# Values of attention heads 2 and 3 computed in one pass of 512-column products, with their weights kept

## The chip, the cores and the metric

The kernel runs on one core of a Trainium2 chip. The metric is the device time of one execution in microseconds. TensorE (PE) does the matrix products, ScalarE (ACT) casts and activations, VectorE (DVE) and GpSimd (POOL) elementwise work; SyncE (SP) issues the transfers that matter here.

## The reference

One layer of an encoder block on 1024 tokens of 1024 features: a combined input projection, gated linear attention in two directions (4 heads, key size 128, value size 256), a pooling branch, a gated merge, and an FFN. The part that the change touches is the value projection of heads 2 and 3 and what is put around it:

```python
h = rmsnorm(x, norm_mix[l])
proj = h @ w_in[l]
q, k, v, r, lr_f, lr_b, u, g_a, g_b = jnp.split(proj, split_points, axis=-1)
...
vh = to_heads(v, GLA_HEADS)
...
scores = jnp.einsum('bhncd,bhnsd->bhncs', q_e, k_e)
scores = jnp.where(mask, scores, 0.0)
o_intra = jnp.einsum('bhncs,bhnse->bhnce', scores, v)
kv = jnp.einsum('bhnsd,bhnse->bhnde', k_d, v)
...
o = (o * jax.nn.silu(r.astype(jnp.float32))).astype(x.dtype)
y_a = o @ w_branch_gla[l]
```

## The kernel before

**Products.** Every large product is made three times in a reduced-precision fp32 format: each operand is split into a hi part and a lo part, and hi x hi, hi x lo and lo x hi are summed in PSUM (`products`, L274; `mm3` calls it and then the queue, see below). The split is made by `split_to`: a cast on ACT (L200) gives hi, a subtraction gives lo (L201, on POOL for weights, on DVE for data). A token tile is 128 tokens (8 of them, `t`), a k-tile is 128 of the 1024 features (8 of them). One `mm3` of 512 columns is one unit of the queue.

**The queue.** TensorE's order is fixed when the program is written. After each `mm3`, `pump(dt)` (dt = 1 for 512 columns, 0.5 for 256) advances several lists:

- `side`: the attention of a head, a generator that yields after each piece how many units to wait until the next. `begin(attention(h, q, k))` puts it in. It first makes decays and their exponentials (its prelude, about 35 units, among them `qe` and `fac` on POOL, L809 and L810, scans on DVE, L778, exponentials on ACT, L798 to L800, key transposes `kp` on PE, L826), then waits until the values of its head are there (`while h not in v_heads: yield 0.5`), then makes 7 backward steps (`advance`, 1.2 units each: the product `kv`, the state `st` on DVE, L838 and L840, and its scaled copies `sb`, `sf`, `so` on ACT, L844 and L848), the scores (`sc`, `p`) and 8 forward steps (`op` in PSUM, the last product of each taking the scaled state `sf`, L922). About 59 units in all.
- `pending`: weight splits of the next projection, one popped every two units. `prepare` loads a weight (raw tiles, 4 buffers) and queues its splits; `take` hands out a weight, makes its remaining splits at once, and prepares the next one.
- `aside`: the work of `branch_jobs` (sums of the branch's weights: `wsum` on POOL, L706), advanced only while `pending` is empty, at a spacing given in units.

All engines work in the order in which the instructions are written, so a split or cast stands behind whatever was written before it on its engine.

**Heads.** The values of heads 0 and 1 are made together by `pair_products` (512 columns: 256 for each head), with attention(0) beside them; their results are split by two casts on ACT (L507) and two subtractions on DVE (L509) for each token tile. Then, for h = 1, 2, 3, `project_qk` makes q and k (2 x 16 units), `begin(attention(h, ...))` queues the head's attention, and for h = 2 and 3 `values` makes the head's own values, 8 tiles of 8 k-tiles with 256 columns each. In this manner attention(0) runs beside the pair products and head 1's projection, attention(1) beside head 2's projection and values, attention(2) beside head 3's.

**The r stage** follows: 8 weights of 128 columns (`j`), 2 halves of 8 units each. From j = 3 on each half is gated (`gated`: Silu on ACT, L1097, four transposes on PE, L1100, a product on DVE, L1107); the halves of j < 3 are stored and gated later (`put_by`). attention(3) runs into this stage.

Of the kernel before, what the change touches and what calls it, by code (L numbers as in the profile page):

```python
# [10 lines left out]
F32 = mybir.dt.float32  # L11
# [42 lines left out]
def kernel(  # L54
# [38 lines left out]
    def name(s):  # L93
        count[0] += 1
        return f"{s}_{count[0]}"

    def slot(dtype=F32, shape=(2, HALF), s="slot"):
        return slots.tile([P, *shape], dtype, tag="slot", name=name(s))
# [10 lines left out]
    def bank(pool, s="ps"):  # L109
        return pool.tile([P, HALF], F32, tag=pool.name, name=name(s))  # L110

    def as_f32(ap):
        return ap.bitcast(F32)
# [85 lines left out]
    def split_to(hi, lo, src, eng=nc.vector):  # L199
        nc.scalar.copy(hi, src)  # L200
        eng.tensor_tensor(lo, src, as_f32(hi), op=ALU.subtract)  # L201
# [35 lines left out]

    order = []
    for h in range(HEADS):
        cols_of = [(Q0 + h * DK, DK), (K0 + h * DK, DK), (V0 + h * DV, DV)]  # L240
        order += [(w_in, KT, *c) for c in cols_of[: 2 if h < 2 else 3]]
    order += [(w_in, KT, R0 + j * P, P) for j in range(KT)]
    order = iter(order)
    loaded, ready = [], []
# [14 lines left out]
    def take(ahead=True):  # L259

        if not ready:
            prepare()
        w = ready.pop(0)
        w.finish()
        if ahead:
            prepare()
        return w
# [8 lines left out]
    def mm3(ps, a, b, first, last, onto=False):  # L276
        products(ps, a, b, first, last, onto)
        pump(ps.shape[-1] / HALF)
# [15 lines left out]
    def tokens(pair, t):  # L294
        return tuple(p[:, (t % 4) * P : (t % 4 + 1) * P] for p in pair)
# [123 lines left out]
            norm_x(t)  # L419
            yield 2  # L420

    def values(w, v, t):
        ps = bank(ps_mm)
        for kt in range(KT):
            mm3(ps[:, :DV], tokens(hT(kt, t // 4), t), w(kt), kt == 0, kt == KT - 1)
        split_to(*(part[:, t % 4, :] for part in v[t // 4]), ps[:, :DV])

    lw = [wts.tile([P, 4, 4, 2 * RANK], F32R, tag="wh", name=name("lw")) for _ in range(2)]
    up = slot(F32R, (HEADS, 2, DK), "up")

    def low_rank_weights():
# [3 lines left out]
            nc.vector.tensor_tensor(lw[i][:, :, 3, :], raw, as_f32(lw[i][:, :, 0, :]), op=ALU.subtract)  # L438
        nc.scalar.copy(up[:, :, :, :], uraw[:, :, :, :])
        nc.vector.tensor_tensor(up[32:64], uraw[32:64], as_f32(up[32:64]), op=ALU.subtract)  # L440

    def value_slots():
        return [(slot(F32R, (4, DV), "vh"), slot(F32R, (4, DV), "vl")) for _ in range(2)]

    cols = const.tile([P, 40], F32, tag="cols", name="cols")

# [41 lines left out]
    split_pair_weight()  # L488
    for kp in range(2):
        transpose_tile(trs[kp], xn[1], 1, kp)  # L490
    pair_v = [[], []]

    def pair_products(ts, before=None):
        banks = [bank(ps_mm) for _ in ts]
        for k in range(KT):
            if before:
                before(k)
            for ps, t in zip(banks, ts):
                mm3(ps[:, :], tokens(hT(k, t // 4), t), pair_w[k], k == 0, k == KT - 1)
        for ps, t in zip(banks, ts):  # L500
            for h in range(2):
                if t // 4 == len(pair_v[h]):
                    pair_v[h].append((slot(F32R, (4, DV), "vh"), slot(F32R, (4, DV), "vl")))
            parts = [[part[:, t % 4, :] for part in v[t // 4]] for v in pair_v]
            halves = [ps[:, h * DV : (h + 1) * DV] for h in range(2)]
            for (hi, _), src in zip(parts, halves):
                nc.scalar.copy(hi, src)  # L507
            for (hi, lo), src in zip(parts, halves):
                nc.vector.tensor_tensor(lo, src, as_f32(hi), op=ALU.subtract)  # L509

    def first_steps(k):
        if k == 2:
# [214 lines left out]
    v_heads, o_heads, unscaled = {}, {}, []  # L727
    HOLD, SCORES = 4.4, 6

    def project_qk():  # L730
        q = slot(s="q")
        k = slot(s="k")
        for dst, scale in ((q, DK**-0.5), (k, 1.0)):
            w = take()
            for half in range(2):
                ps = feature_major(w, hT, half)
                nc.scalar.activation(dst[:, half, :], ps[:, :], AF.Copy, scale=scale)
        return q, k
# [220 lines left out]
    def first_qk():  # L959
        q, k = slot(s="q"), slot(s="k")  # L960
        low_rank(0)
        weights = [take()]
        for half in range(2):
            if half:
                finish_side()
                low_rank(1)
                prepare()
            for n, (dst, scale) in enumerate(((q, DK**-0.5), (k, 1.0))):
                if n == len(weights):
                    weights.append(take(ahead=False))  # L970
                ps = feature_major(weights[n], hT, half)
                nc.scalar.activation(dst[:, half, :], ps[:, :], AF.Copy, scale=scale)
        return q, k

    for h in range(HEADS):
        qk = project_qk() if h else first_qk()
        begin(attention(h, *qk))
        if h == 0:
            for ts in ((7,), (6,), (5, 4)):
                pair_products(ts)  # L980
            v_heads.update(enumerate(pair_v))
            prepare_beside(map(branch_jobs, range(4)), 5)
        if h > 1:
            v = value_slots()
            w = take()
            for t in range(NT):
                values(w, v, t)
            v_heads[h] = v

    class Unit:  # L990

# [1041 lines left out]
```

## Time and profile before

| | us |
|---|---|
| median of 3 runs | 1380.25 (1379.61 to 1381.26) |
| the profiled execution | 1380.1 |
| its span | 1378.1 |
| TensorE busy | 1367.6 |
| values of head 2 begin on TensorE | 154.3 |
| first gated Silu on ACT | 321.8 |

In a row of the timeline stand the start in us from the span's start, the duration, engine, line, operation, output and inputs, the shapes, how many rows were joined (x), and in brackets how long the engine had been idle and what released it. Durations of matmuls are pipelined latencies, so they overlap; the distance between two starts is what a product costs.

### The profile page before, as it was taken

The page shows a single profiled execution, that of the slowest core. Times are in us where ns is not written, and L with a number is a line of the kernel's source. Part 1 is how long each engine was busy: PE and PEld are TensorE (multiplying, and loading weights), DVE is VectorE, ACT ScalarE, POOL GpSimd, SP SyncE. Part 2 cuts the span into 40 slices and gives each one's busy share as a digit, 9 for nine tenths or more (in the row PEclk, how much of TensorE's full clock was granted, in tenths as well). Part 3 has the DMA queues.
Part 4 walks back from the last instruction along what each step waited for, and adds up shares of the span by engine and source line. Part 5 has one row for each costly group of instructions (what it writes and reads, how often), then busy time and mean ns, then how long its engine had stood idle before and what let it go on. Part 6 is the DMA issues. An engine that isn't in the chain of part 4 may idle for free. (4 is left out here: it accounts for less than half of the span.)

```text
span 1378.1 us, 18207 instructions
## 1 busy us (share of the span) xinstructions
PE 1367.6 (99%) x6514; PEld 1147.4 (83%) x6514; DVE 839.8 (61%) x1027; ACT 642.6 (47%) x1170; POOL 750.7 (54%) x554
## 2 busy tenths in 40 slices
PE   9999999999999999999999999999999999999998
PEld 7888899988888888888888888888888888888886
DVE  6364656557745876688883955656656556343375
ACT  7375666655334445554347533333333334444353
POOL 3222617132297646668665276666666667455454
PEclk9999999999999999999999999999999999999999
DMA  6121413312478678996516355555544447985561
GB/s 226 31 62 47 147 62 125 110 48 77 138 230 278 197 229 277 371 394 216 175 61 245 115 176 176 176 176 176 165 143 139 144 136 266 385 306 186 170 214 77
DMA packets 166586, 243.60 MB, mean 177 GB/s; under 512 B 10936, under 2 KB 95968, under 8 KB 166496
## 3 DMA queue, kind: packets, MB, share of 16 engines
q1 hardware_dynamic: 166352, 242.18, 52.3%
q8 instruction: 51, 0.84, 0.3%
q14 instruction: 39, 0.32, 0.1%
q10 hardware_dynamic: 144, 0.26, 0.1%
HBM read 164.55 MB, written 77.86 MB: 176 GB/s over the span
## 5 line engine op out<-in xcount | busy, mean ns | idle before, releaser
L201 POOL TENSOR_TENSOR wl<-fs,wh 128x512 fp32r<-128x512 f32 x120 | 167.6, 1400 | 157.2 <-ACT wh L200 103.2
L274 PE MATMUL ps<-gh,wh 128*128 128x512 f32 x616 | 240.9, 391 | 0.0
L274 PE MATMUL ps<-gl,wh 128*128 128x512 f32 x616 | 240.2, 390 | 0.3 <-DVE gl L1591 0.3
L274 PE MATMUL ps<-gh,wl 128*128 128x512 f32 x616 | 240.0, 390 | 0.0
L201 POOL TENSOR_TENSOR wl<-fraw,wh 128x512 fp32r<-128x512 f32 x90 | 129.7, 1441 | 63.6 <-ACT wh L200 61.2
L274 PE MATMUL ps<-hh,wh 128*128 128x512 f32 x376 | 151.9, 404 | 0.0
L201 POOL TENSOR_TENSOR ol<-gor,oh 128x1024 fp32r<-128x1024 f32 (+1 forms) x42 | 101.7, 2425 | 85.7 <-ACT oh L200 59.6
L274 PE MATMUL ps<-hh,wl 128*128 128x512 f32 x376 | 146.9, 391 | 0.0
L274 PE MATMUL ps<-hl,wh 128*128 128x512 f32 x376 | 146.8, 390 | 0.0
L274 PEld LDWEIGHTS ps<-gl,wh 128*128 128x128 f32 x616 | 115.8, 188 | 24.1 <-DVE gl L1591 0.7
L274 PEld LDWEIGHTS ps<-gh,wh 128*128 128x128 f32 x616 | 115.8, 188 | 24.0 <-ACT hb L1610 0.3
L274 PEld LDWEIGHTS ps<-gh,wl 128*128 128x128 f32 x616 | 115.7, 188 | 24.1
L201 POOL TENSOR_TENSOR wl<-raw,wh 128x512 fp32r<-128x512 f32 x40 | 54.7, 1379 | 121.9 <-ACT wh L200 103.5
L274 PE MATMUL ps<-oh,oh 128*128 128x512 f32 x308 | 120.0, 390 | 0.0
L274 PE MATMUL ps<-oh,ol 128*128 128x512 f32 x308 | 120.0, 390 | 0.0
L274 PE MATMUL ps<-ol,oh 128*128 128x512 f32 x308 | 120.0, 389 | 0.0
L201 POOL TENSOR_TENSOR wl<-wraw,wh 128x512 fp32r<-128x512 f32 x56 | 92.2, 1675 | 44.7 <-ACT wh L200 44.5
L201 DVE TENSOR_TENSOR ol<-wor,oh 128x1024 fp32r<-128x1024 f32 (+1 forms) x42 | 62.8, 1506 | 68.1 <-ACT oh L200 55.5
L200 ACT CAST wh<-fs 128x512 fp32r<-128x512 f32 x120 | 73.8, 615 | 26.1 <-DVE fs L1010 25.1
L274 PEld LDWEIGHTS ps<-hh,wl 128*128 128x128 f32 x376 | 70.6, 188 | 15.0
L274 PEld LDWEIGHTS ps<-hl,wh 128*128 128x128 f32 x376 | 70.9, 188 | 12.9
L274 PEld LDWEIGHTS ps<-hh,wh 128*128 128x128 f32 x376 | 70.8, 188 | 12.8
(279 smaller groups left out, 3126.3 us busy)
## 6 DMA issues: line engine op xcount, KB each, us to landing
fraw<-in_w_ffn_in_dram SPq DMA_DIRECT2D x44, 512.0 KB, 7.2
gor<-g_out SPq DMA_DIRECT2D x35, 512.0 KB, 5.8
g_out<-s SPq DMA_DIRECT2D x44, 256.0 KB, 2.3
raw<-in_w_in_dram SPq DMA_DIRECT2D x40, 256.0 KB, 5.1
fraw<-in_w_in_dram SPq DMA_DIRECT2D x20, 512.0 KB, 7.1
wor<-t_out SPq DMA_DIRECT2D x20, 512.0 KB, 4.5
g_out<-g SPq DMA_DIRECT2D x33, 256.0 KB, 2.5
x<-in_x_dram SPq DMA_DIRECT2D x16, 512.0 KB, 4.5
```

Of the source, the lines that this page charges most:

```text
L200: nc.scalar.copy(hi, src)
L201: eng.tensor_tensor(lo, src, as_f32(hi), op=ALU.subtract)
L274: nc.tensor.matmul(ps, a[i], b[j], start=first and n == 0, stop=last and n == 2, skip_group_check=onto)
```

## The change

The values of heads 2 and 3 are computed in one pass behind head 2's q and k projection. `ValueWeights` loads eight k-tiles of 512 columns (256 KB each), four of them when head 2's k-projection begins and the others as splits are made; it splits six of them while that projection runs (through `pending`) and the last two in the first token tile. Two of the k-tiles (6 and 7) are kept in slots, because the pools `wh` and `wl` have six buffers. `products` makes 8 token tiles of 8 products of 512 columns, from t = 7 to t = 0, and `keep_values` (also used by `pair_products`) splits each result into the values of the two heads. The q weights of head 3 are prepared in the last token tile (t = 0, third k-tile) instead of a whole projection ahead. attention(2) is queued ahead of the products but gets its values only when all are made; attention(3) is queued behind head 3's projection, with the r stage right behind. The branch jobs are queued as two and two, spaced 3.7 and 4 units instead of 5. In all 384 products of 256 columns become 192 of 512.

```diff
@@ -237,8 +237,7 @@
 
     order = []
     for h in range(HEADS):
-        cols_of = [(Q0 + h * DK, DK), (K0 + h * DK, DK), (V0 + h * DV, DV)]
-        order += [(w_in, KT, *c) for c in cols_of[: 2 if h < 2 else 3]]
+        order += [(w_in, KT, c + h * DK, DK) for c in (Q0, K0)]
     order += [(w_in, KT, R0 + j * P, P) for j in range(KT)]
     order = iter(order)
     loaded, ready = [], []
@@ -419,15 +418,6 @@
             norm_x(t)
             yield 2
 
-    def values(w, v, t):
-        ps = bank(ps_mm)
-        for kt in range(KT):
-            mm3(ps[:, :DV], tokens(hT(kt, t // 4), t), w(kt), kt == 0, kt == KT - 1)
-        split_to(*(part[:, t % 4, :] for part in v[t // 4]), ps[:, :DV])
-
-
-
-
     lw = [wts.tile([P, 4, 4, 2 * RANK], F32R, tag="wh", name=name("lw")) for _ in range(2)]
     up = slot(F32R, (HEADS, 2, DK), "up")
 
@@ -438,9 +428,6 @@
             nc.vector.tensor_tensor(lw[i][:, :, 3, :], raw, as_f32(lw[i][:, :, 0, :]), op=ALU.subtract)
         nc.scalar.copy(up[:, :, :, :], uraw[:, :, :, :])
         nc.vector.tensor_tensor(up[32:64], uraw[32:64], as_f32(up[32:64]), op=ALU.subtract)
-
-    def value_slots():
-        return [(slot(F32R, (4, DV), "vh"), slot(F32R, (4, DV), "vl")) for _ in range(2)]
 
     cols = const.tile([P, 40], F32, tag="cols", name="cols")
 
@@ -488,7 +475,18 @@
     split_pair_weight()
     for kp in range(2):
         transpose_tile(trs[kp], xn[1], 1, kp)
-    pair_v = [[], []]
+    pair_v = {}, {}
+
+    def keep_values(vs, t, ps):
+        for v in vs:
+            if t // 4 not in v:
+                v[t // 4] = slot(F32R, (4, DV), "vh"), slot(F32R, (4, DV), "vl")
+        parts = [[part[:, t % 4, :] for part in v[t // 4]] for v in vs]
+        halves = [ps[:, h * DV : (h + 1) * DV] for h in range(2)]
+        for (hi, _), src in zip(parts, halves):
+            nc.scalar.copy(hi, src)
+        for (hi, lo), src in zip(parts, halves):
+            nc.vector.tensor_tensor(lo, src, as_f32(hi), op=ALU.subtract)
 
     def pair_products(ts, before=None):
         banks = [bank(ps_mm) for _ in ts]
@@ -498,15 +496,7 @@
             for ps, t in zip(banks, ts):
                 mm3(ps[:, :], tokens(hT(k, t // 4), t), pair_w[k], k == 0, k == KT - 1)
         for ps, t in zip(banks, ts):
-            for h in range(2):
-                if t // 4 == len(pair_v[h]):
-                    pair_v[h].append((slot(F32R, (4, DV), "vh"), slot(F32R, (4, DV), "vl")))
-            parts = [[part[:, t % 4, :] for part in v[t // 4]] for v in pair_v]
-            halves = [ps[:, h * DV : (h + 1) * DV] for h in range(2)]
-            for (hi, _), src in zip(parts, halves):
-                nc.scalar.copy(hi, src)
-            for (hi, lo), src in zip(parts, halves):
-                nc.vector.tensor_tensor(lo, src, as_f32(hi), op=ALU.subtract)
+            keep_values(pair_v, t, ps)
 
     def first_steps(k):
         if k == 2:
@@ -727,11 +717,64 @@
     v_heads, o_heads, unscaled = {}, {}, []
     HOLD, SCORES = 4.4, 6
 
-    def project_qk():
+    class ValueWeights:
+
+
+        ORDER = (0, 1, 2, 3, 6, 7, 4, 5)
+        IN_SLOTS = (6, 7)
+
+        def __init__(self):
+            self.raw, self.parts = [], {}
+            for _ in range(4):
+                self.load()
+            pending.append(self.split)
+            pending.extend([self.next] * 5)
+
+        def load(self):
+            k = self.ORDER[len(self.raw)]
+            raw = wts.tile([P, HALF], F32, tag="raw", name=name("raw"), bufs=4)
+            nc.sync.dma_start(raw[:, :], w_in[k * P : (k + 1) * P, V0 + 2 * DV : V0 + 4 * DV])
+            self.raw.append(raw)
+
+        def split(self):
+            n = len(self.parts)
+            k = self.ORDER[n]
+            if k in self.IN_SLOTS:
+                w = slot(F32R, s="wv")
+                parts = w[:, 0, :], w[:, 1, :]
+            else:
+                parts = [wts.tile([P, HALF], F32R, tag=s, name=name(s))[:, :] for s in ("wh", "wl")]
+            split_to(*parts, self.raw[n][:, :], nc.gpsimd)
+            self.parts[k] = parts
+
+        def next(self):
+            if len(self.raw) < KT:
+                self.load()
+            self.split()
+
+        def products(self):
+            while pending:
+                pending.pop(0)()
+            vs = {}, {}
+            for t in reversed(range(NT)):
+                ps = bank(ps_mm)
+                for n, k in enumerate(self.ORDER):
+                    if t == NT - 1 and n in (0, 1):
+                        self.next()
+                    elif t == 0 and n == 2:
+                        prepare()
+                    mm3(ps[:, :], tokens(hT(k, t // 4), t), self.parts[k], n == 0, n == KT - 1)
+                keep_values(vs, t, ps)
+            return vs
+
+    def project_qk(last=False):
         q = slot(s="q")
         k = slot(s="k")
         for dst, scale in ((q, DK**-0.5), (k, 1.0)):
-            w = take()
+            final = last and dst is k
+            w = take(not final)
+            if final:
+                value_weights.append(ValueWeights())
             for half in range(2):
                 ps = feature_major(w, hT, half)
                 nc.scalar.activation(dst[:, half, :], ps[:, :], AF.Copy, scale=scale)
@@ -972,20 +1015,18 @@
                 nc.scalar.activation(dst[:, half, :], ps[:, :], AF.Copy, scale=scale)
         return q, k
 
+    value_weights = []
     for h in range(HEADS):
-        qk = project_qk() if h else first_qk()
+        qk = project_qk(h == 2) if h else first_qk()
         begin(attention(h, *qk))
         if h == 0:
             for ts in ((7,), (6,), (5, 4)):
                 pair_products(ts)
             v_heads.update(enumerate(pair_v))
-            prepare_beside(map(branch_jobs, range(4)), 5)
-        if h > 1:
-            v = value_slots()
-            w = take()
-            for t in range(NT):
-                values(w, v, t)
-            v_heads[h] = v
+            prepare_beside(map(branch_jobs, range(2)), 3.7)
+        if h == 2:
+            v_heads.update(zip((2, 3), value_weights.pop().products()))
+            prepare_beside(map(branch_jobs, range(2, 4)), 4)
 
     class Unit:
```

**POOL at the values of head 2.** Rows of the program before, from the split of the first value weights of head 2 (`wl`) through attention(1)'s `qe` and `fac`; `wsum` is the branch's work, the last two `wl` belong to head 3's q weights.

```order
L201 TENSOR_TENSOR wl_1554<-raw_1501,wh_1553 128x512
L201 TENSOR_TENSOR wl_1576<-raw_1503,wh_1575 128x512
L706 TENSOR_TENSOR wsum_1453<-wsum_1453 128x512
L809 TENSOR_TENSOR qe_1562<-qe_1562,q_982 128x512
L810 TENSOR_TENSOR fac_1563<-fac_1563 128x4
L706 TENSOR_TENSOR wsum_1453<-wsum_1452,wsum_1453 128x512
L809 TENSOR_TENSOR qe_1562<-qe_1562,q_982 128x512
L810 TENSOR_TENSOR fac_1595<-fac_1595 128x4
L809 TENSOR_TENSOR qe_1522<-qe_1522,q_982 128x512
L810 TENSOR_TENSOR fac_1645<-fac_1645 128x4
L201 TENSOR_TENSOR wl_1685<-raw_1629,wh_1684 128x512
L201 TENSOR_TENSOR wl_1722<-raw_1631,wh_1721 128x512
```

The same place of the changed program, from the fourth lo part of the value weights (the third and a `qe` with its `fac` stand right ahead); `wv` are the k-tiles that are kept in slots.

```order
L201 TENSOR_TENSOR wl_1567<-raw_1506,wh_1566 128x512
L201 TENSOR_TENSOR wv_1590<-raw_1525,wv_1590 128x512
L852 TENSOR_TENSOR qe_1575<-qe_1575,q_982 128x512
L853 TENSOR_TENSOR fac_1576<-fac_1576 128x4
L201 TENSOR_TENSOR wv_1603<-raw_1548,wv_1603 128x512
L696 TENSOR_TENSOR wsum_1374<-wsum_1375,wsum_1374 128x512
L696 TENSOR_TENSOR wsum_1374<-wsum_1374 128x512
L852 TENSOR_TENSOR qe_1575<-qe_1575,q_982 128x512
L853 TENSOR_TENSOR fac_1612<-fac_1612 128x4
L201 TENSOR_TENSOR wl_1647<-raw_1564,wh_1646 128x512
L201 TENSOR_TENSOR wl_1666<-raw_1588,wh_1665 128x512
```

The splits of the value weights now reach on through this stretch, and the last two of them (k-tiles 4 and 5) stand behind two `wsum` and two `qe`.

**ACT at the end of the products.** In the program before, head 3's q weights (`wh_2180`) are cast ahead of attention(2)'s exponentials (L798 to L800):

```order
L758 ACTIVATE z_2136<-z_2136 128x512
L200 CAST wh_2180<-raw_2151 128x512
L764 ACT_TABLE_LOAD
L764 ACTIVATE z_2093<-z_2093 128x512
L764 ACTIVATE z_2110<-z_2110 128x512
L764 ACTIVATE z_2124<-z_2124 128x512
L764 ACTIVATE z_2136<-z_2136 128x512
L200 CAST wh_2196<-raw_2153 128x512
```

In the changed program they (`wh_2252`, `wh_2262`) stand behind the exponentials of its last run:

```order
L487 CAST vh_2096<-ps_2150 128x256
L487 CAST vh_2098<-ps_2150 128x256
L200 CAST kt_2239<-kp_2234 128x512
L841 ACTIVATE qe_2132<-z_2041 128x512
L842 ACTIVATE z_2041<-z_2041 128x512
L843 ACTIVATE fac_2242<-tot_2217 128x8
L200 CAST wh_2252<-raw_2224 128x512
L200 CAST wh_2262<-raw_2226 128x512
```

**ACT at the end of attention(3), in the r stage.** Before, its last forward steps (`sf`, `so`, and the squares of `op`) are all made ahead of the first Silu (`sr`):

```order
L844 ACTIVATE sf_3405<-st_3410,fac_3079 128x256
L924 ACTIVATE op_3400,oms_3246<-op_3400 128x256
L924 ACTIVATE op_3419,oms_3246<-op_3419 128x256
L1144 COPY r_3188<-ps_3265 128x512
L200 CAST wh_3459<-raw_3431 128x512
L200 CAST wh_3469<-raw_3433 128x512
L1097 ACT_TABLE_LOAD
L1097 ACTIVATE sr_3479<-r_2920 128x512
L1097 ACTIVATE sr_3489<-ps_3435 128x512
```

In the changed program the table load and two Silu stand ahead of the last scaled state (`sf_3272`), which the last `op` product takes:

```order
L887 ACTIVATE sf_3230<-st_3235,fac_2919 128x256
L891 ACTIVATE so_3238<-st_3235,fac_2919 128x256
L967 ACTIVATE op_3225,oms_3086<-op_3225 128x256
L1138 ACT_TABLE_LOAD
L1138 ACTIVATE sr_3243<-r_2670 128x512
L1138 ACTIVATE sr_3253<-ps_3077 128x512
L887 ACTIVATE sf_3272<-st_3277,fac_2919 128x256
L967 ACTIVATE op_3267,oms_3086<-op_3267 128x256
L967 ACTIVATE op_3286,oms_3086<-op_3286 128x256
```

## The prediction

> **What bounds the kernel now.** I read the page first, then the waits of TensorE, then the products by shape, then the timeline around the two heads whose values change.
>
> ```profile
> span 1378.1 us, 18207 instructions
> PE 1367.6 (99%) x6514; PEld 1147.4 (83%) x6514; DVE 839.8 (61%) x1027; ACT 642.6 (47%) x1170; POOL 750.7 (54%) x554
> PE 44%; DVE 1%; ACT 1%; issue 0%; POOLq 0%; POOL 0%; DVEq 0%; ACTq 0%
> ```
>
> TensorE is busy 99% of the span and is the largest share of the chain that ended last: all the others together hold a few per cent of it. Whatever shortens TensorE's own stream shortens the time; whatever makes it wait lengthens it. Its waits in the stretch from the second head to the last are short:
>
> ```profile
> PE kp L826 <- DVE ke L808: 0.5, 1, 0.5
> PE op L274 <- DVE p L201: 0.4, 2, 0.2
> PE sc L856 <- DVE st L840: 0.2, 1, 0.2
> ```
>
> So there is almost nothing to win from waits, and much to lose: each new one adds in full.
>
> **The stream.** The products that the change replaces, grouped by shape between 154 and 290 us; there are three such groups of 128, one for each hi/lo pairing (the mean is a latency; what counts is the distance of starts):
>
> ```profile
> L274 PE MATMUL ps<-wh,hh 128*128 128x256 f32 x128 | 40.0, 312 | 0.0
> L922 PE MATMUL op<-sb,qe 128*128 128x256 f32 x28 | 8.3, 379 | 0.0
> ```
>
> Starts of the 256-column form, first within a product and then behind a plain fp32 product (L922):
>
> ```profile
> 250.06 0.28 PE L274 MATMUL ps<-wh,hh 128*128 128x256 f32 x1
> 250.18 0.29 PE L274 MATMUL ps<-wl,hh 128*128 128x256 f32 x1
> ...
> 251.57 0.59 PE L922 MATMUL op<-sf,qe 128*128 128x256 f32 x2
> 251.81 0.47 PE L274 MATMUL ps<-wh,hh 128*128 128x256 f32 x1
> 252.12 0.28 PE L274 MATMUL ps<-wl,hh 128*128 128x256 f32 x1
> ```
>
> The same two distances of the 512-column form, from the projections:
>
> ```profile
> 123.10 0.58 PE L274 MATMUL ps<-hh,wh 128*128 128x512 f32 x1
> 123.52 0.39 PE L274 MATMUL ps<-hl,wh 128*128 128x512 f32 x1
> ...
> 132.97 0.39 PE L274 MATMUL ps<-hh,wh 128*128 128x512 f32 x1
> 133.20 0.39 PE L274 MATMUL ps<-hl,wh 128*128 128x512 f32 x1
> ```
>
> 256 columns take 0.120 us, 512 columns 0.227; behind a plain fp32 product they take 0.31 and 0.42, so 0.19 and up to 0.19 more. Over other such places the 512-column surcharge is smaller; I bound it by 0 and 0.19 and take 0.09. Before: 3 x 128 = 384 products, of which some 20 stand behind a fp32 one (estimated from 28 + 28 L922 products of the two heads, of which two in three are followed by an attention product instead): 384 x 0.120 + 20 x 0.19 = 49.9 us. After: 192 x 0.227 + 20 x 0.09 = 45.4. **Stream: -4.5 us** (-2.5 to -6.3).
>
> [...]
>
> **Waits that go.** In the old values of head 2, TensorE lost time here:
>
> ```profile
> 154.53 0.28 PE L274 MATMUL ps<-wh,hl 128*128 128x256 f32 x1
> 155.29 0.66 PE L826 MATMUL kp<-ident,ke 128*128 128x128 f32 x4 [0.49 <-DVE ke L808]
> ```
>
> 155.29 - 154.53 - 0.12 = 0.64 us; with the score and `op` waits above, each with its refill of the pipeline, some 2.0 us (1.1 if only the listed waits count, 2.5 if every irregular distance does). The same work now meets a TensorE that comes later for another reason (next part), and finds it done: **-2.0**.
>
> **First tile: the weight splits on POOL.** This is the term that decides. Before, the value weights of a head were four tiles split one per two units. Now both heads need eight (k-tiles 0 to 7), six popped during the 16 units of head 2's k-projection and two in the first tile of products, and all eight are used within the first eight units (7 x 0.68 = 4.8 us, five attention steps of 0.36 and the key transposes of 0.5 put between: 154.3 + 4.8 + 1.8 + 0.5 = 161.4, when TensorE without a wait asks for the last). What POOL and ACT did in that stretch before:
>
> ```profile
> 141.91 2.73 SPq L208 DMA_DIRECT2D raw<-in_w_in_dram  x4
> ```
>
> ```profile
> 147.88 0.62 ACT L200 CAST wh<-raw 128x512 fp32r<-128x512 f32 x1 [4.14 <-DMA raw<-in_w_in_dram]
> 148.52 1.28 ACT L798 ACT_TABLE_LOAD   x1
> 150.92 1.13 ACT L200 CAST wh<-raw 128x512 fp32r<-128x512 f32 x2
> ```
>
> ```profile
> 151.61 1.29 POOL L201 TENSOR_TENSOR wl<-raw,wh 128x512 fp32r<-128x512 f32 x1 [1.74 <-ACT wh L200]
> 152.85 2.20 POOL L809 TENSOR_TENSOR qe<-qe,q 128x512 f32<-128x512 f32 x1
> 155.01 0.20 POOL L810 TENSOR_TENSOR fac<-fac 128x4 f32<-128x4 f32 x1
> 155.17 2.55 POOL L201 TENSOR_TENSOR wl<-raw,wh 128x512 fp32r<-128x512 f32 x2
> 157.64 1.32 POOL L706 TENSOR_TENSOR wsum<-wsum 128x512 f32<-128x512 f32 x1
> 158.90 2.23 POOL L809 TENSOR_TENSOR qe<-qe,q 128x512 f32<-128x512 f32 x1
> ```
>
> Loads are issued at 141.9 and the first cast starts at 147.88; one write less stands ahead of them on SP's queue now, so I put the first cast up to 1 us earlier. The order of ACT has two casts, then the table load and two exponentials (to about 150.5 to 151.4), then the third cast (0.6): POOL begins the third lo part at 151.1 to 152.0. From there POOL, strictly in its order, has eleven operations of 1.26 us (two took 2.55 above, with a little overlap) to the last lo part (third lo, `qe`, lo, lo, `qe`, lo, two `wsum`, `qe`, lo, lo) and three `fac` of 0.15: 13.9 + 0.45 = 14.3 us. Two of the `qe` took 2.2 instead of 1.3 before, beside this scan on DVE and its twin at 158.3:
>
> ```profile
> 152.25 1.73 DVE L778 TENSOR_TENSOR_SCAN z<-carry,la 128x512 f32<-128x512 bf16 x1
> ```
>
> That adds 0 to 1.9. The last lo part is done at 151.1 + 14.3 = 165.4 at the earliest and 152.0 + 14.3 + 1.9 = 168.2 at the latest, against 161.4: a wait of 4.0 to 6.8. I take **+5.5**. Behind the waiting product stands everything on TensorE; ACT and DVE only get ahead by it, which is why the old waits go.
>
> **Tile boundary in attention(1)'s last forward step.** Two casts and two subtractions instead of one each stand ahead of the state update that the next `op` product needs. One more cast and one more subtraction, by these rows:
>
> ```profile
> 89.82 1.34 ACT L507 CAST vh<-ps 128x256 fp32r<-128x256 f32 x4 [0.80 <-PE ps L274]
> 163.57 0.42 DVE L201 TENSOR_TENSOR vl<-ps,vh 128x256 fp32r<-128x256 f32 x1 [1.00 <-ACT vh L200]
> ```
>
> 1.34/4 + 0.42 = 0.76, with the releases **+0.8** (0 if TensorE's units between cover it).
>
> **Start of head 3's q-projection.** Its weights are now prepared in the last product tile, six units ahead, where they used to be 32 ahead. ACT's cast of them stands behind the exponentials of attention(2)'s last run, which stand behind a scan. The nearest such end of a prelude is that of attention(0):
>
> ```profile
> 91.65 0.59 ACT L200 CAST kt<-kp 128x512 fp32r<-128x512 f32 x1 [0.48 <-PE kp L826]
> 92.91 0.60 ACT L798 ACTIVATE qe<-z 128x512 f32<-128x512 f32 x1 [0.67 <-DVE z L789]
> ```
>
> There the first key transposes ran at 87.8, and the exponentials end at 92.91 + 1.2 = 94.1, 6.3 us after them. Now two value subtractions (0.8) stand ahead of that scan: 7.1; cast 0.62, 7.7; lo part 1.29 on POOL, 9.0. TensorE comes after eight units and two transposes, 8 x 0.68 + 0.9 = 6.4, and needs the lo part 0.46 later: 9.0 - 6.9 = 2.1, or 3.5 if the scan takes the 1.73 of the row above instead of the 1.23 it took there and the lo part is slowed like `qe`. **+2.7**. The transfer is no part of it: its loads are issued units before the cast.
>
> **Attention(3) meets the r stage's gates.** Attention(3) now starts with the r stage, some ten units later against it than before, and ends at about unit 59, while the first gated r tile comes at unit 56. On ACT a table load and two Silu, on DVE two gating products, stand ahead of the state of the last step:
>
> ```profile
> 320.51 1.28 ACT L1097 ACT_TABLE_LOAD   x1
> 321.80 0.63 ACT L1097 ACTIVATE sr<-r 128x512 f32<-128x512 f32 x1
> ```
>
> 1.28 + 2 x 0.63 + 2 x 0.68 (gating, costed as DVE's other 512-column products) + 0.48 + 0.51 for state and scaled state = 4.9 us, of which TensorE covers 3.1 (eight transposes, a product of 0.68, two `op` groups): **+1.8** (0 to 2.5).
>
> 192 matmuls fewer also mean 192 weight loads fewer; those lie under the products (PEld 83%), at nothing. The 8 loads of 256 KB replace 8 of the same size. The branch sums are spaced otherwise, but stand on POOL and DVE behind no TensorE wait other than the one counted.
>
> **Sum**, against the profiled execution's 1380.1 (span 1378.1 and 2.0 around it, 0.15 under the median): -4.5 - 2.0 + 5.5 + 0.8 + 2.7 + 1.8 = +4.3; 1384.4, by the median **1384.5 us**.
>
> **Rivals.**
> *Both weight waits are hidden* (faster). POOL has the last lo part before 161.4 and head 3's q weights before TensorE. For it: POOL is busy 54%, and the first cast may come earlier. Against: fourteen in-order operations in 14 us. -4.5 - 2.0 + 0.8 + 1.8 = -3.9: 1376.3.
> *Even.* All waits at their small end: 4.0, 2.1, 0.5 at the boundary, 0.5 at the gates: -6.5 + 7.1 = +0.6, 1380.9. For it: ACT's cast may come early and POOL miss both scans.
> *All at their large end*: 6.8 + 0.8 + 3.5 + 2.5 - 6.5 = +7.1, 1387.4. For it: two of four `qe` were slowed before.
> *The width gains nothing*: the narrow form costs 0.120 only for what stands around it, so 384 narrow take as long as 192 wide; then +2.5 more, 1387.0. Against it: the distance is steady at 0.12 over whole products. [...]
>
> **How the numbers follow.** Forecast 0.41 (1382.5 to 1386.5), even 0.22, hidden 0.17, large end 0.15, width 0.05. A measurement of this kernel can tell 0.2% (2.8 us), so slower begins at 1383.0 and faster at 1377.5. Slower: 0.41 less 0.02 under the bound, plus 0.15 and 0.05: 0.59; same 0.22 + 0.02 = 0.24; faster 0.17. The range 1377.0 to 1388.0 leaves out most of the hidden case and the far tail; the forecast's own range is 1382.5 to 1386.5.
>
> **What would show it.** Starts of the value products 0.227 apart and 192 fewer. In the first tile, a wait of TensorE on a lo part from POOL of 4 to 7 us in all, on the fifth to eighth k-tile. A wait of 2 to 3.5 us on a weight at head 3's q-projection. One of 1 to 2.5 us of an `op` product on ACT's scaled state at the first gate. The forecast is wrong if the lo parts of the first tile stand ready, or if TensorE waits anywhere else for over 2 us.

## The result, and the profile after

The changed kernel takes 1393.38 us (median of five, 1392.49 to 1394.02) against 1379.61 for the kernel before (median of five): a ratio of 1.0099, 95% interval 1.0084 to 1.0113. It is slower, by 13.8 us, where +4.3 was forecast and 1388.0 was the end of the range. The way was right, the size was three times as large.

The head of the page of the changed kernel, and the first line of its chain:

```profile
span 1390.6 us, 17833 instructions
PE 1368.6 (98%) x6322; PEld 1138.4 (82%) x6322; DVE 837.3 (60%) x1027; ACT 642.8 (46%) x1170; POOL 749.3 (54%) x554
PE 43%; DVE 1%; ACT 1%; issue 0%; POOLq 0%; POOL 0%; DVEq 0%; ACTq 0%
```

TensorE has 192 instructions fewer and yet is busy 1.0 us longer: that is the first sign of something else than waits. The span is 12.5 us longer. From the r stage's end on, the same products run in both traces at a constant distance of 12.1 us, so all of it lies ahead of 350 us.

What TensorE waited for, in the whole span (engine, output, line, releaser: us in total, times, longest):

```profile
PE ps L273 <- POOL wl L201: 4.7, 3, 3.9
PE ps L273 <- ACT wh L200: 2.5, 1, 2.5
PE op L965 <- ACT sf L887: 2.1, 2, 1.7
PE ps L273 <- POOL wv L201: 1.7, 1, 1.7
...
PE kp L869 <- DVE ke L851: 0.5, 2, 0.3
PE op L273 <- ACT p L200: 0.4, 1, 0.4
```

The first four rows are the four waits of the forecast, in their places: lo parts from POOL (the 4.7 are 3.87 in the first tile, 0.62 at head 3's q weights and 0.2 behind 350 us), head 3's q weights from ACT, the scaled state `sf` twice. The last two are old waits that were to go.

TensorE in the first value tile (start, duration, and in brackets the wait):

```profile
159.63 0.39 PE L273 MATMUL ps<-wv,hh 128*128 128x512 f32 x1
161.70 0.50 PE L273 MATMUL ps<-wv,hh 128*128 128x512 f32 x1 [1.67 <-POOL wv L201]
...
162.62 0.39 PE L273 MATMUL ps<-wh,hh 128*128 128x512 f32 x1
166.88 0.80 PE L273 MATMUL ps<-wl,hh 128*128 128x512 f32 x1 [3.87 <-POOL wl L201]
...
168.54 0.63 PE L273 MATMUL ps<-wh,hh 128*128 128x512 f32 x1
168.97 0.63 PE L273 MATMUL ps<-wl,hh 128*128 128x512 f32 x1
...
172.99 0.39 PE L273 MATMUL ps<-wl,hh 128*128 128x512 f32 x1
173.22 0.40 PE L273 MATMUL ps<-wh,hl 128*128 128x512 f32 x1
```

By the starts, less the 0.227 of a product, the two waits cost 1.84 and 4.03 us, 5.9 together. Then look at the distances behind the long one: 168.97 - 168.54 = 0.43 us for a product that takes 0.227 elsewhere, with nothing in brackets; at 172.99 the distance is 0.23 again. The same stretches by windows (PE busy, granted clock, DMA share, GB/s) say why:

```profile
162.00:166.00 4.00, 1.01 (x6) 1.00 0.34 131
166.00:170.00 4.00, 3.12 (x9) 0.51 0.00 0
170.00:174.00 4.00, 4.00 (x18) 0.63 0.00 0
174.00:178.00 4.00, 4.00 (x28) 1.00 0.02 4
```

The granted clock of TensorE falls to half in the last 0.8 us of the long wait and comes back some 6 us after it: it is 0.50 from 166.09 to 172.92 us. From 166.88 to 172.99 stand nine 512-column starts, six 256-column ones and four transposes, some 3.3 us at the usual distances; they took 6.1. So this wait cost 2.8 us more than its own length. No transfer runs there (DMA share 0.00), and the forecast had no such term.

The tile boundary in attention(1), head 3's q-projection, and the last `op` product, which stands behind the gates:

```profile
200.00 0.28 PE L273 MATMUL op<-vh,p 128*128 128x256 f32 x1
200.75 0.70 PE L965 MATMUL op<-sf,qe 128*128 128x256 f32 x2 [0.47 <-ACT sf L887]
...
228.82 0.39 PE L273 MATMUL ps<-wh,hl 128*128 128x512 f32 x1
231.69 0.50 PE L273 MATMUL ps<-hh,wh 128*128 128x512 f32 x1 [2.48 <-ACT wh L200]
232.03 0.40 PE L273 MATMUL ps<-hl,wh 128*128 128x512 f32 x1
233.04 0.50 PE L273 MATMUL ps<-hh,wl 128*128 128x512 f32 x1 [0.62 <-POOL wl L201]
...
335.10 0.28 PE L273 MATMUL op<-vh,p 128*128 128x256 f32 x1
337.05 0.70 PE L965 MATMUL op<-sf,qe 128*128 128x256 f32 x2 [1.67 <-ACT sf L887]
```

By the starts 0.6 us at the boundary (forecast 0.8), 2.64 + 0.78 = 3.4 us for the q weights (forecast 2.7) and 1.8 for the gates (forecast 1.8).

POOL in the first tile shows the queue that the forecast counted:

```profile
151.98 1.30 POOL L201 TENSOR_TENSOR wl<-raw,wh 128x512 fp32r<-128x512 f32 x1 [1.15 <-ACT wh L200]
153.24 2.21 POOL L852 TENSOR_TENSOR qe<-qe,q 128x512 f32<-128x512 f32 x1
...
158.07 1.28 POOL L852 TENSOR_TENSOR qe<-qe,q 128x512 f32<-128x512 f32 x1
159.32 1.11 POOL L853 TENSOR_TENSOR fac<-fac 128x4 f32<-128x4 f32 x1
160.39 1.26 POOL L201 TENSOR_TENSOR wv<-raw,wv 128x512 fp32r<-128x512 f32 x1
161.61 1.29 POOL L696 TENSOR_TENSOR wsum<-wsum,wsum 128x512 f32<-128x512 f32 x1
162.97 1.26 POOL L696 TENSOR_TENSOR wsum<-wsum 128x512 f32<-128x512 f32 x1
164.19 1.26 POOL L852 TENSOR_TENSOR qe<-qe,q 128x512 f32<-128x512 f32 x1
...
165.56 2.49 POOL L201 TENSOR_TENSOR wl<-raw,wh 128x512 fp32r<-128x512 f32 x2
```

From 151.98 to 168.05 POOL has no idle time; the last lo part is done at 168.05, within the forecast's 165.4 to 168.2. TensorE has in fact two waits there because the sixth k-tile (`wv`), too, stands behind a `qe` and a `fac`.

### The profile page after: what moved, and what is told of

Its sections match the earlier page's. It is cut to its first block, busy times and chain, and to the rows that moved or that the text cites. A ratio compares the mean times of both kernels' runs of the same rounds, so it can differ in the third digit from the quotient of the medians.

```text
span 1390.6 us, 17833 instructions
## 1 busy us (share of the span) xinstructions
PE 1368.6 (98%) x6322; PEld 1138.4 (82%) x6322; DVE 837.3 (60%) x1027; ACT 642.8 (46%) x1170; POOL 749.3 (54%) x554
## 5 line engine op out<-in xcount | busy, mean ns | idle before, releaser
L201 POOL TENSOR_TENSOR wl<-fs,wh 128x512 fp32r<-128x512 f32 x120 | 168.2, 1405 | 156.1 <-ACT wh L200 102.0
L201 POOL TENSOR_TENSOR wl<-raw,wh 128x512 fp32r<-128x512 f32 x38 | 51.1, 1357 | 133.6 <-ACT wh L200 126.0
```

## The experiments

Twelve kernels were run. Differences are of medians; the kernel before, timed beside them, had medians of 1379.7, 1379.7 and 1379.4 in the three groups.

### Each wait by itself

**fill.** Spare products inside the long wait:

```diff
+                    if t == NT - 1 and n == 6:
+                        spare = bank(ps_mm, "spare")
+                        for _ in range(3):
+                            products(spare[:, :], tokens(hT(0, 1), t), self.parts[0])
                     mm3(ps[:, :], tokens(hT(k, t // 4), t), self.parts[k], n == 0, n == KT - 1)
```

> The changed kernel with nine spare products of 512 columns, whose result nobody reads, put ahead of the seventh k-tile of the first value tile, inside the 3.9 us in which TensorE waited for the lo part from POOL. Theory A (a long wait makes the products behind it slow, at 0.43 us a start instead of 0.227, for some 6 us): the lo part comes at the same 166.8 us, the wait falls to about 1.9 us, the starts behind it stay 0.227 apart, and the time falls by the 3.0 us of the slow stretch, 1393.4 to about 1390.4. Theory B (the slow stretch comes from what else runs at that place, ports or transfers): starts stay 0.43 apart, 1393.4. Theory C (POOL is not the limit and the spare products only push everything back): 1395.4.

Measured: 1392.73 us (1391.28 to 1393.27), hardly faster. The windows of its trace at the first tile and at head 3's q-projection:

```profile
164.00:168.00 4.00, 2.15 (x10) 1.00 0.17 67
168.00:172.00 4.00, 4.00 (x25) 1.00 0.00 0
...
228.00:232.00 4.00, 2.65 (x8) 0.76 0.16 41
232.00:236.00 4.00, 4.00 (x20) 0.81 0.32 90
```

The long wait in the first tile fell to 1.9 us and the clock there stayed at 1.00: theory A holds at this place. But now the wait at head 3's q-projection, as long as before (2.5 and 0.6 us), is followed by a lowered clock (0.76 and 0.81 in these rows), where it was 1.00 in the profile of the changed kernel. So it isn't the length of a wait alone. Executions of one and the same kernel differ, too: this one took 1391.28 at a mean granted clock of 0.998 and 1392.5 to 1393.3 at 0.996 and 0.997.

**wsum_later.**

```diff
-            prepare_beside(map(branch_jobs, range(2)), 3.7)
...
-            prepare_beside(map(branch_jobs, range(2, 4)), 4)
+            prepare_beside(map(branch_jobs, range(4)), 4)
```

> The changed kernel with all four branch jobs queued behind the value products, so that no wsum stands on POOL between the value weights. Theory A (the first-tile wait is POOL's queue): the last two lo parts come 2.5 us earlier, the wait of 3.9 us falls to about 1.4, no slow stretch follows, 1393.4 - 2.5 - 3.0 = about 1388. Theory B (the lo parts wait for casts or transfers, POOL only shows it): wait and slow stretch stay, 1393.4.

Measured: 1385.82 us (1385.40 to 1386.94), 7.6 faster than the changed kernel: more than theory A. POOL was the limit, and a second thing came with it. The first cast of value weights on ACT, in the changed kernel

```profile
147.59 1.29 ACT L200 CAST wh<-raw 128x512 fp32r<-128x512 f32 x2 [4.02 <-DMA raw<-in_w_in_dram]
```

and in wsum_later:

```profile
145.00 1.26 ACT L200 CAST wh<-raw 128x512 fp32r<-128x512 f32 x2 [1.19 <-DMA raw<-in_w_in_dram]
```

The raw weights land 2.6 us earlier when the branch jobs do not run ahead of them, so that the wait on `wv` goes altogether and that on `wl` falls to 1.3 us. POOL's last lo part is then done at 162.97 instead of 168.05 us: 2.6 us sooner by the earlier weights, 2.5 by the two `wsum` that are gone, so the run does not price POOL's order alone. Why the weights land earlier was not taken apart: SP issues them 1.9 us earlier (140.4 instead of 142.3); the branch jobs' own transfers are not beside them in the changed kernel either (DMA share 0.00 from 136 to 138 us in both). What theory A did not foresee is that the wait at head 3's q-projection, again 2.5 us, is followed by a lowered clock in this trace: 0.63 from 224 to 228 us and 0.94 in the four behind it.

**two_tiles.**

```diff
-            for t in reversed(range(NT)):
-                ps = bank(ps_mm)
+            for ts in ((7, 6), (5,), (4,), (3,), (2,), (1,), (0,)):
+                banks = [bank(ps_mm) for _ in ts]
                 for n, k in enumerate(self.ORDER):
+                    for ps, t in zip(banks, ts):
...
```

> The changed kernel with the first two value tiles (t = 7 and 6) made together, k-tile by k-tile in two PSUM banks, so that each new k-tile is asked for only every two units. Theory A: the waits on the fifth to eighth k-tile (5.9 us) fall to under 1 us and the slow stretch of 3.0 us goes with them; some of the old waits of attention(1) (2 us) may come back: 1385 to 1387. Theory B (the lateness of POOL is passed on to a later place, as tile boundary or attention waits): over 1390.

Measured: 1388.41 us (1388.23 to 1388.66), between the two. The first tile has no wait on POOL any more, but the q-projection of head 3 waits longer, and the clock behind it is low:

```profile
PE ps L273 <- ACT wh L200: 3.6, 1, 3.6
```

The granted clock is 0.70 from 224 to 228 us and 0.50 in the four behind it. Part of the 8.7 us that were taken away came back there: TensorE comes there 6.9 us sooner (its last value product starts at 221.94 instead of 228.82), and attention(2)'s last exponentials, ahead of the cast, only 5.7 (224.19 instead of 229.93).

**q3_early.**

```diff
-                    elif t == 0 and n == 2:
-                        prepare()
+                    elif t == 0 and n in (2, 3):
+                        if n == 2:
+                            prepare()
+                        pending.pop(0)()
```

> The changed kernel with the two splits of head 3's q weights written at the third and fourth k-tile of the last value tile, ahead of attention(2)'s last exponentials on ACT, instead of two units apart behind them. Theory A (the cast stands behind the exponentials): the waits of 2.5 us on ACT's cast and 0.6 us on POOL's lo part go, 1393.4 - 3.4 = about 1390.0. Theory B (the weights' transfer is late, or the exponentials, now later, make attention(2) wait as long): 1392.5 to 1393.4.

Measured: 1388.41 us (1388.25 to 1388.87), 5.0 faster than the changed kernel, 1.6 more than the wait itself. Both waits on the q weights are gone, only two short ones of 0.2 us came in their place, and with them goes a slow stretch that most executions of the changed kernel seem to have had at that place (their clock is 0.995 to 0.996; here it is 0.996 to 0.997). The profile of gate_later below, which has the changed kernel's q weights, shows it: at a mean clock of 0.995 it has two slow stretches, one at the first tile (clock 0.97, 0.50 and 0.67 in the rows of 4 us from 160 to 172) and one right behind this wait (0.57 from 232 to 236 us).

**fill_q3**, fill and q3_early together:

> The changed kernel with the nine spare products of fill (their result is read by nobody) and the early q splits of q3_early. The lo parts come from POOL as late as in q3_early; only the longest wait is cut from 3.9 to about 1.9 us by products that do nothing. Theory A (a wait of nearly 4 us lowers the granted clock behind it, in fill the wait at head 3's q-projection did it instead): no stretch with a granted clock under 1, q3_early's 1388.4 - 3.0 = about 1385.4. Theory B (the slow stretch has another cause): a slow stretch stays somewhere, 1388.

Measured: 1387.98 us (1387.28 to 1388.71), 0.4 below q3_early. In its trace no 4 us of the stretch up to 400 us has a clock under 0.995, and from the values on it is 1.5 us ahead of q3_early, although the lo parts come no sooner. The other executions tell the price: 1387.28 and 1387.48 at clocks of 1.000 and 0.999, 1388.47 and 1388.71 at 0.998. Some 1.2 us for a slow stretch that comes in some executions and not in others. So cutting the longest wait did not exclude a slow stretch: in the profile TensorE still stands idle for 1.7 us from 160 to 164 and for 1.9 from 164 to 168, and no slow stretch follows, but by their clocks two executions of four have one. Theory A's 1385.4 was too low: in q3_early's trace the slow stretch cost 2.1 us and not 3.0 (fill_q3 is 0.57 us behind it at the late lo part and 1.53 ahead from 172 us on), because TensorE stood idle in part of it (the clock is 0.60 from 164 to 168 us, and the wait lasts to 166.56). By the time alone theory B's 1388 fits; that a slow stretch stays is not so in this trace.

**gate_later.**

```diff
-                put_by()
-                gated(j, half, ps[:, :])
+                if j == BY and half == 0:
+                    soon(5, put_by, partial(gated, j, half, ps[:, :]))
+                else:
+                    put_by()
+                    gated(j, half, ps[:, :])
```

> The changed kernel with the first two gatings of the r stage (one stored half, one of j = 3) put off by five units, so that the table load, the two Silu and the two gating products stand behind attention(3)'s last step on ACT and DVE. Theory A (they stand ahead of the state that the last op product takes): the wait of 1.7 us on the scaled state goes, 1393.4 - 1.8 = about 1391.6. Theory B (the wait moves to the put-off gating, or to the PSUM bank that it holds five units longer): 1393 to 1394.

Measured: 1391.08 us (1390.58 to 1392.20), 2.3 faster. The wait of 1.7 us is gone, and the put-off gating waits for nothing: theory A.

### All of them, and what is left

**all_three** joins two_tiles, q3_early and gate_later.

> The changed kernel with the first two value tiles together, head 3's q splits early and the gatings later. Theory A (the loss is these three waits and the slow stretches that follow the long ones; without them only the gain of the stream is left): two_tiles' 1388.4 less its waits at head 3's q-projection (4.3), its slow stretch (3.4) and the gate's wait (1.8) = about 1378.9, a little below the kernel before, and no stretch with a granted clock under 1. Theory B (the wide products lose somewhere that is no wait): 1382 or more.

Measured: 1381.78 us (1381.08 to 1382.31), ratio to the kernel before 1.0015 (1.0006 to 1.0023). The granted clock is 0.999 and no stretch is slow; 11.6 of the 13.8 us are gone. But it is 2.1 us slower than the kernel before where it should have been a little faster: theory A is right on the waits and wrong on what remains. Its waits between 100 and 345 us:

```profile
PE sc L903 <- DVE st L887: 0.8, 3, 0.3
PE op L273 <- DVE p L201: 0.7, 3, 0.2
PE kp L873 <- DVE ke L855: 0.6, 2, 0.3
PE op L969 <- ACT sf L891: 0.5, 1, 0.5
PE op L273 <- ACT p L200: 0.4, 1, 0.4
PE kv L273 <- DVE st L885: 0.3, 1, 0.3
PE kv L273 <- DVE kt L201: 0.2, 1, 0.2
```

3.5 us, against 1.1 in the kernel before. All are short, and all are of attention's own chain: key transposes, states, scores.

**all_t5.**

```diff
-                    keep_values(vs, t, ps)
+                    if t == 5:
+                        soon(1.5, partial(keep_values, vs, t, ps))
+                    else:
+                        keep_values(vs, t, ps)
```

> all_three, with the split of value tile t = 5 put off by 1.5 units, so that its two casts and two subtractions stand behind the state of attention(1)'s last step. Theory A: the wait of 0.6 us on the scaled state there goes, all_three - 0.6. Theory B (the split is then late for its PSUM bank): no gain.

Measured: 1380.85 us (1380.16 to 1381.56), 0.9 below all_three; the wait on `sf` is gone. Ratio to the kernel before 1.0007 (0.9998 to 1.0016).

**all_halves.**

```diff
-                        mm3(ps[:, :], tokens(hT(k, t // 4), t), self.parts[k], n == 0, n == KT - 1)
+                        for half in range(2):
+                            c = slice(half * DV, (half + 1) * DV)
+                            products(
+                                ps[:, c], tokens(hT(k, t // 4), t), tuple(p[:, c] for p in self.parts[k]),
+                                n == 0 and half == 0, n == KT - 1 and half == 1, True,
+                            )
+                        pump(1)
```

> all_three, with each 512-column value product made as two of 256 columns into the halves of the same bank, everything else in the same place. It prices the width by itself. By the trace's distances (0.120 and 0.227): 384 x 0.120 - 192 x 0.227 = 2.5 us slower than all_three. [...]

Measured: 1381.55 us (1381.09 to 1382.02), no slower than all_three. Yet the distances are what they were, 0.12 and 0.23, in all_halves

```profile
176.75 0.28 PE L273 MATMUL ps<-wl,hh 128*128 128x256 f32 x1
176.87 0.28 PE L273 MATMUL ps<-wh,hl 128*128 128x256 f32 x1
```

and in all_three, where a product behind a plain fp32 one (L969) is also to be seen:

```profile
175.72 0.38 PE L969 MATMUL op<-sb,qe 128*128 128x256 f32 x1
175.75 0.58 PE L273 MATMUL ps<-wh,hh 128*128 128x512 f32 x1
176.16 0.39 PE L273 MATMUL ps<-wl,hh 128*128 128x512 f32 x1
176.39 0.39 PE L273 MATMUL ps<-wh,hl 128*128 128x512 f32 x1
```

Summed by the starts over all value products, less their waits, they take 48.2 us in all_halves and 46.3 in all_three: 1.8 of the 2.5 us are there on TensorE, and are not kept. The profiled spans are 0.5 us apart (1380.3 and 1379.8), and by the medians all_halves is no slower. At head 3's q-projection all_halves is 1.1 us behind all_three (the same product at 223.94 and 222.87 us); from 236 us on it is 0.2 us ahead (up to a wait on scores at 299.5 us), because all_three then waits 0.30 us on the state of a `kv` bank and 0.30 on scores, and all_halves on neither:

```profile
228.43 0.36 PE L273 MATMUL kv<-vh,kt 128*128 128x256 f32 x1 [0.30 <-DVE st L885]
234.25 0.60 PE L903 MATMUL sc<-qe,ke 128*128 128x128 f32 x3 [0.30 <-DVE st L887]
```

**slack**, **before_slack** and **slack_wsum** give attention more units between its pieces, on all_t5, on the kernel before, and on all_t5 with wsum_later:

```diff
-    HOLD, SCORES = 4.4, 6
+    HOLD, SCORES = 4.4, 7
...
+        yield 0.6
         p = scores(0)
         yield SCORES
```

> all_t5 with attention given more time: SCORES 7 units instead of 6, 0.6 units ahead of the first scores, the split of tile t = 5 put off by 4 units and the first gatings by 7. Theory A (what the faster stream gains is given back in short waits of attention's pieces, whose distance is counted in units of TensorE's products): the waits on p (1.1 us) and on the states ahead of the scores (0.5 us) go, all_t5's 1380.85 - 1.5 = about 1379.3. Theory B (the waits move to other pieces of the same chain): 1380.5 to 1381.

> The kernel before with the same two numbers of attention (SCORES 7, 0.6 units ahead of the first scores), without the change. Theory A: its waits on p and ahead of the scores (0.6 us listed, some 1.4 by the starts) go too, 1379.7 - 1.0 = about 1378.7, so that slack is no gain of the change. Theory B (its narrow products leave enough time as it is): 1379.7.

> slack, with all four branch jobs behind the value products, so that POOL is ahead with the value weights and the decays of attention(1). Theory A (POOL is no limit any more once two tiles share the k-tiles): same as slack within 0.5. Theory B (short waits on the key transposes and states come from POOL's lateness): 1 us faster.

Measured: slack 1379.98 (1379.17 to 1380.26), ratio to the kernel before 1.0002 (0.9993 to 1.0011); before_slack 1379.92 (1.0005, 0.9996 to 1.0014); slack_wsum 1380.62 (1.0012, 1.0003 to 1.0020). Each set against the kernel before that was timed beside it, slack is 0.6 us above and all_t5 1.2, so slack takes 0.6 of the 1.5 us, and the two intervals overlap: neither theory is decided. The waits on `p` fall from 1.1 to 0.2 us, but 0.5 us on a q weight's lo part and 0.7 more on key transposes come in. On the kernel before the same numbers gain nothing. That is the time of theory B, but not its reason: it now has waits on `p` of 1.5 us where it had 0.4, so they moved and grew. slack_wsum is no faster than slack, so nothing shows POOL as a limit any more; it is even 0.6 us slower, a little outside theory A's 0.5, and five of its eleven executions took 1381.6 to 1382.4 us at a mean clock of 0.998.

None of the twelve is faster than the kernel before; slack is level with it. Whether a longer search over attention's distances would bring the 2 us of the stream out was not tried.

## Why the prediction was wrong

Sums are of the profiled executions, 12.1 us at the end of the r stage.

| step | forecast | in the trace |
|---|---|---|
| first tile, weights from POOL | +5.5 | +5.9 |
| slow stretch behind it | none | +2.8 |
| start of head 3's q-projection | +2.7 | +3.4 |
| gates ahead of attention(3)'s last step | +1.8 | +1.8 |
| tile boundary in attention(1) | +0.8 | +0.6 |
| old waits that go | -2.0 | +0.2 (1.1 listed before, 1.3 after) |
| stream | -4.5 | -2.6 (what is left) |

**The four new waits** were right in place, cause and size: 11.7 us where 10.8 were forecast. wsum_later, q3_early, gate_later and all_t5 took each of them away by taking away the named cause (wsum_later all but 1.3 us, and half of it by weights that landed earlier). The rivals with small or hidden waits fell.

**The step that failed first is that a wait was priced at its own length.** The forecast wrote that TensorE waits and everything behind it stands, and then went on at full speed. The trace shows a granted clock of 0.51 and 0.63 in the 8 us from 166 us on, where the long wait ends, and 0.43 us a product there instead of 0.227. The profiles hold these waits of TensorE and this clock behind them:

| trace | place | waits, us | granted clock |
|---|---|---|---|
| changed kernel | first tile | 1.67, 3.87 | 0.50 from 166.09 to 172.92 us |
| changed kernel | head 3's q-projection | 2.48, 0.62 | 1.00 from 228 to 236 us |
| fill | first tile | 1.7, 1.9 | 1.00 from 160 to 176 us |
| fill | head 3's q-projection | 2.5, 0.6 | 0.76, 0.81 (228 to 232, 232 to 236 us) |
| wsum_later | first tile | 1.3 | 1.00 from 160 to 176 us |
| wsum_later | head 3's q-projection | 2.5, 0.6 | 0.63, 0.94 (224 to 228, 228 to 232 us) |
| two_tiles | head 3's q-projection | 3.6 | 0.70, 0.50, 0.95 (224 to 228, 228 to 232, 232 to 236 us) |
| q3_early | first tile | 1.7, 3.9 | 0.60, 0.54 (164 to 168, 168 to 172 us) |
| gate_later | first tile | 1.7, 3.9 | 0.97, 0.50, 0.67 (160 to 164, 164 to 168, 168 to 172 us) |
| gate_later | head 3's q-projection | 2.5, 0.6 | 0.57 (232 to 236 us) |

With each of the four waits of 3.6 us or more the clock was low, and where the longest was 1.3 or 1.9 us it stayed at 1.00. Behind the pair of 2.5 and 0.6 us the clock was low in three traces and full in that of the changed kernel. What made that difference no run shows.

The median lies 0.9 us above the profiled execution (1392.49, the fastest of the five, at clock 0.997 where the others have 0.995 and 0.996), and the kernel before has no such difference: by the clocks, another slow stretch. Of the 9.5 us between forecast and median, about 3.7 are this step. The two gains that did not come, the stream and the old waits, are as much: 6.5 were forecast and 2.4 found, 4.1 us less. The four waits add 0.9.

**The stream** was mis-sized. Of the width's 2.5 us, 1.8 are found when all value products are summed (all_halves against all_three). The 2.0 us for products behind a plain fp32 one were not there. The surcharge is 0.19 us behind an `op` product of plain fp32 for both widths that follow (0.306 instead of 0.120, 0.418 instead of 0.227), and not the 0.09 that the forecast took in the middle for the wide ones; 0.08 stand behind transposes and scores. And it goes with attention's products, which the change leaves as they are: from 100 us to the end of attention(3), 54 products stand behind such an `op` product before and 52 in all_three. Fewer of them are value products (7 instead of 16), but more belong to projections (21 instead of 14), which the forecast did not count.

**The old waits that go** were only moved: key transposes still wait 0.5 us, and two waits on `p` and one on scores stand in the r stage. The forecast took the lateness of TensorE as cover for them. In attention(1) that held for scores and `p`; that they come back at attention(3) because TensorE is no longer late there is argued, not tested.

**Beyond the forecast**: all_three, all_halves and slack show that even without the large waits the change is worth nothing here. The rival in which the width gains nothing is wrong by the starts and right by the time. Faster products shorten the units in which attention's pieces are spaced, and ACT and DVE, whose steps take their own time, then make TensorE wait: the waits listed are 3.5 us in all_three and 2.4 in all_halves, and of the 1.8 us of the width at most 0.5 reach the end (spans of 1380.3 and 1379.8). That the spacing is the cause is argued from this: slack, which was to remove it, moved the waits and did not end them.

## What to carry to other kernels

Where an engine is busy 99% of the time, price a new wait in two parts: its length, and what runs slow behind it; a wait of nearly 4 us cost 2.8 us more here. In the profiles each wait of 3.6 us or more had a lowered clock with it, and waits of 2.5 and 0.6 us close together had one in three profiles of four: the second part of the price came in some executions only. Filling a wait (fill_q3), or letting two tiles share each new weight (two_tiles), removed that part at its place in the profiles. Count the in-order queues ahead of a late operand one instruction at a time: that gave all four waits within 0.7 us. And before a stream is made faster, look whether the work beside it is spaced in its units: here the gain came back as short waits, and the slack that was tried moved them.

## What the runs showed of the hardware

A wait of 3.87 us was followed by products at 0.43 us instead of 0.227 for 6.1 us. The granted clock was 0.50 from 166.09 to 172.92 us there. Waits of 2.48 and 0.62 us were followed by a clock of 1.00 in the changed kernel's trace, and waits of 2.5 and 0.6 us by a lowered one in fill's (0.76 and 0.81 in two rows of 4 us), wsum_later's (0.63 and 0.94) and gate_later's (0.57 in one). A product behind a plain fp32 `op` product took 0.19 us more, for 256 columns and for 512. The first cast of value weights, which their transfer released, started at 147.59 us with the branch jobs queued ahead and at 145.00 without them. On POOL a `fac` of four columns, 0.2 us in the median of 16, took 1.11 at 159.3 us, beside a scan on DVE that ran from 158.70 to 160.45.
